# The last 256 tokens of a two-layer trunk: residual by unit-matrix products, output as token rows, and a 7-operation root

## The chip, the cores and the metric

The kernel runs on one core of a Trainium2 chip. A core has a matrix engine (TensorE, PE in the profile; its weight loads are PEld), three elementwise engines (VectorE = DVE, ScalarE = ACT, GpSimd = POOL), and DMA queues, which here are fed by the sync engine (SP) and by POOL. Matrix products are written to banks of PSUM, everything else lies in SBUF on 128 partitions. The metric is the time of one execution in microseconds (us), as the median of several runs.

## The reference

One sequence of 512 tokens with 1024 features passes two layers and a final norm.

```python
for layer in range(2):
    h = rms_norm(x, ln1[layer])
    # layer 0: RWKV-7 time mixing, 12 heads of 64; layer 1: chunk attention, 12 heads
    # both: 4 heads of attention into 256 memory tokens, on rms_norm(mem, mem_norm)
    x = x + concatenate([mix, mo]) @ w_out[layer]
    x = x + conv_glu(rms_norm(x, ln2[layer]), ffn_in[layer], ..., ffn_out[layer])
return rms_norm(x, ln_f)     # x * rsqrt(mean(x * x) + 1e-6) * ln_f
```

`conv_glu` is a gated unit with a three-tap convolution over tokens: (gelu(conv(gate)) * val) @ ffn_out, with 2816 inner features, which are 22 tiles of 128.

## The kernel before

**Layout.** Activations stand with features on partitions: `xT` holds 8 tiles (`KD`) of 128 features x 512 tokens (`S`). A weight is loaded as float32 (`wraw`, two buffers), copied by ACT into a rounded high part `whi` (L170), and DVE (L178) makes the low part `wlo` by subtraction. `dense` then issues three kinds of products into one bank: high x high (L216), high weight x low activation (L217), and, at the end of the bank's series, low weight x high activation (L220).

**Norms.** `acc` collects the squares of the tiles. `norm_steps` multiplies 128-token blocks of it with a matrix of 1/1024 (L270), which puts the mean of each token on a partition, adds 1e-6 (L272), takes the reciprocal root, copies each root along 128 columns (L278), turns the blocks on PE (L283), and copies the result from the bank to `rho` (L284), in which every partition holds the factor of each token. `rsqrt_small` (L237 to L245) starts from an integer estimate and does three Newton rounds of three operations, ten DVE operations in all. `head_rsqrt` does the same for the norms of the heads in layer 0 (sums L906, copy L912, turn L915). The norm of the memory rows (`mrc`, L275) goes through `norm_steps` as well.

**Order.** The work is written as generators, which `weave` interleaves by stated costs; a scheduler with its own model of the engines then fixes the order of the instructions on each engine. Layer 0 runs in stages of 128 mixer features (`prepare`): projections, head norm of the keys, the operands `AR` and `KB` (L991, L995, L999) and 16 pairs of score products from them (L1005). The scores leave over SP by DMA, come back as `Lr`, and after the scan's small products as `Tc` (L1051), which L1144 and L1153 use. The first stage's score products stand next to the keys and values of memory (L884 to L886). The feed-forward parts are held in the order in which they are written.

**The end.** `finish` makes the last feature tile in two halves of 256 tokens. `half(u)` is one series of products into a 128x256 bank. `store(u)` multiplies the bank by `rho` (L1662), adds it to `xT` (L1663), squares on ACT (L1665), scales by `ln_f` on ACT (L1666), adds the squares to `acc` (L1667), runs the norm of these 256 tokens (`norm_rho`), and makes four output tiles of two feature tiles each (L1674), each sent by a DMA on SP (L1676). The store of the first half is woven into the products of the second, and the second store comes after them. The output in memory has partition, feature tile and token as its axes, and the host turns it.

## Time and profile before

| | |
|---|---|
| time, median of 3 runs | 1323.93 us (1323.37 to 1325.35) |
| the profiled execution's own time | 1325.66 us |
| its span | 1323.9 us |
| mean granted TensorE clock | 0.996 |
| PE busy | 1293.9 us, 98% of the span |
| DVE busy | 982.2 us, 74% |
| ACT busy | 787.5 us, 59% |
| POOL busy | 113.4 us, 9% |
| DMA traffic | 170.51 MB, mean 129 GB/s |

The busy time of an engine is the sum of its instructions, and it says nothing of which of them the end waited for. The chain of waits does: it starts at the last instruction and goes back, step by step, to whatever released it. A bracket behind an instruction, as in "[2.16 <-DVE tmp L278]", says that its engine had been idle for 2.16 us and that the copy L278 into a `tmp` tile on VectorE ended the wait. The table by stretches cuts the span into pieces of time and gives each engine's busy time in each of them, with the granted clock as a share of full speed. Groups of instructions give the count, the busy sum and the mean in ns of one.

### The profile page before, as it was taken

The numbers are of one execution on the slowest core, as the hardware profiler recorded it, in microseconds if no ns is written. First come the engines' busy times: TensorE is split into PE (matmuls) and PEld (weight loads), VectorE is DVE, ScalarE is ACT, GpSimd is POOL, SyncE is SP. The second block draws the span as 40 slices with busy tenths as digits, with TensorE's granted clock in tenths as the row PEclk, the third lists the DMA queues.
The fourth block names the chain that finished last, engine by engine and source line by source line (L and its number), as shares of the span: only waits on it lengthen the run. The fifth ranks groups of instructions, "written<-read, shape, count | busy, mean of one in ns | idle before, by whom it ended". The sixth has DMA issues, their size and how long they took to land.

```text
span 1323.9 us, 26431 instructions
## 1 busy us (share of the span) xinstructions
PE 1293.9 (98%) x10558; PEld 1121.0 (85%) x10558; DVE 982.2 (74%) x1947; ACT 787.5 (59%) x1316; POOL 113.4 (9%) x133
## 2 busy tenths in 40 slices
PE   9999999999999999999999999999999999999996
PEld 7787777777789999998888878786899999988886
DVE  7967767765699999998344675757989999995335
ACT  6666665665566666777223566657757667674221
POOL 0000000000001211210000000000012112110000
PEclk9999999999999999999999999999999999999998
DMA  6374434451326887775333432332448878854332
GB/s 199 109 189 98 102 81 110 90 113 57 111 81 160 194 187 178 191 160 143 104 105 102 134 104 72 96 112 72 127 114 193 183 174 201 183 129 128 101 88 78
DMA packets 88683, 170.51 MB, mean 129 GB/s; under 512 B 21232, under 2 KB 31600, under 8 KB 88560
## 3 DMA queue, kind: packets, MB, share of 16 engines
q1 hardware_dynamic: 68320, 124.94, 30.7%
q0 software_dynamic: 20240, 43.88, 19.8%
q8 instruction: 83, 1.36, 0.4%
q14 instruction: 40, 0.33, 0.1%
HBM read 152.57 MB, written 6.29 MB: 120 GB/s over the span
## 4 chain that ended last, share of the span: by engine, by line
PE 80%; DVE 6%; ACT 6%; issue 5%; DMA 3%; SPq 0%; POOL 0%; DVEq 0%; ACTq 0%; POOLq 0%
PE psf L393 19%; PE psd L220 11%; PE psd L216 11%; PE psd L217 11%; PE psf L395 9%; PE pss L1570 1%; DMA wlo<-in_ffn_out_dram 1%; PE pss L906 1%; PE pss L1229 1%; PE pss L1240 1%; PE pss L329 1%; PE pss L1556 1%; PE pss L1379 1%; PE pss L1095 1%; PE pss L319 1%
## 5 line engine op out<-in xcount | busy, mean ns | idle before, releaser
L170 ACT CAST whi<-wraw 128x1024 fp32r<-128x1024 f32 (+1 forms) x116 | 118.0, 1020 | 207.8 <-DMA wraw<-in_ffn_out_dram 130.0
L178 DVE TENSOR_TENSOR wlo<-wraw,whi 128x1024 fp32r<-128x1024 f32 (+1 forms) x93 | 109.6, 1179 | 134.0 <-PE psd L220 70.4
L447 ACT CAST whi<-raw 128x1024 fp32r<-128x1024 f32 (+1 forms) x168 | 153.3, 941 | 68.3 <-PE psf L393 31.9
L393 PE MATMUL psf<-tl,whi 128*128 128x256 f32 x672 | 168.8, 283 | 0.0
L393 PE MATMUL psf<-th,whi 128*128 128x256 f32 x672 | 168.6, 283 | 0.0
L452 DVE TENSOR_TENSOR wlo<-raw,whi 128x1024 fp32r<-128x1024 f32 (+1 forms) x126 | 131.5, 1043 | 14.4 <-ACT whi L447 14.1
L393 PEld LDWEIGHTS psf<-tl,whi 128*128 128x128 f32 x672 | 128.9, 192 | 0.0
L393 PEld LDWEIGHTS psf<-th,whi 128*128 128x128 f32 x672 | 128.7, 192 | 0.0
L216 PE MATMUL psd<-r1h,whi 128*128 128x512 f32 x248 | 101.5, 410 | 0.1
L217 PE MATMUL psd<-r1l,whi 128*128 128x512 f32 x248 | 97.8, 395 | 0.0
L395 PE MATMUL psf<-th,wlo 128*128 128x256 f32 x504 | 81.7, 283 | 0.0
L220 PE MATMUL psd<-r1h,wlo 128*128 128x512 f32 x248 | 72.0, 406 | 0.0
L395 PEld LDWEIGHTS psf<-th,wlo 128*128 128x128 f32 x504 | 69.8, 192 | 0.0
L430 POOL DMA_DIRECT2D wlv<-in_ffn_in_dram x40 | 61.3, 1531 | 58.5 <-DVE tmp L514 57.8
L393 PE MATMUL psf<-r1h,whi 128*128 128x256 f32 x252 | 63.5, 284 | 0.7 <-ACT whi L447 0.7
L393 PE MATMUL psf<-r2h,whi 128*128 128x256 f32 x252 | 63.5, 284 | 0.7 <-ACT whi L447 0.7
L393 PE MATMUL psf<-r1l,whi 128*128 128x256 f32 x252 | 63.2, 283 | 0.0
L393 PE MATMUL psf<-r2l,whi 128*128 128x256 f32 x252 | 63.2, 283 | 0.0
L473 ACT ACTIVATE tmp<-tmp,vec 128x512 f32<-128x512 f32 x44 | 35.9, 817 | 37.9 <-DVE tmp L460 36.6
L216 PEld LDWEIGHTS psd<-r1h,whi 128*128 128x128 f32 x248 | 46.6, 188 | 11.9 <-issue 2.8
L217 PEld LDWEIGHTS psd<-r1l,whi 128*128 128x128 f32 x248 | 46.6, 188 | 8.0 <-issue 0.2
L216 PE MATMUL psd<-th,whi 128*128 128x512 f32 (+1 forms) x136 | 51.0, 379 | 2.3 <-ACT whi L170 2.3
(487 smaller groups left out, 3464.8 us busy)
## 6 DMA issues: line engine op xcount, KB each, us to landing
raw<-in_ffn_in_dram SPq DMA_DIRECT2D x42, 512.0 KB, 3.9
raw<-in_ffn_in_dram SPq DMA_DIRECT2D x84, 256.0 KB, 4.3
wlv<-in_ffn_in_dram POOLq DMA_DIRECT2D x40, 512.0 KB, 8.0
wraw<-in_ffn_out_dram SPq DMA_DIRECT2D x32, 448.0 KB, 3.5
wraw<-in_wA_dram SPq DMA_DIRECT2D x20, 512.0 KB, 4.1
wraw<-in_w_out_dram SPq DMA_DIRECT2D x16, 512.0 KB, 3.9
wraw<-in_ffn_out_dram SPq DMA_DIRECT2D x16, 512.0 KB, 3.5
wlo<-in_wA_dram POOLq DMA_DIRECT2D x15, 512.0 KB, 6.6
```

The costliest lines, as they stand in the source:

```text
L170: high = lambda: pin(SC.copy(hi[:, :n], raw))
L178: pin(V.tensor_tensor(lo[:, :n], raw, hi[:, :n], op=ALU.subtract))
L216: PE.matmul(ps, wh[:, j * P:(j + 1) * P], ah, start=start and n == 0, stop=False)
L217: dense_at[0] = PE.matmul(ps, wh[:, j * P:(j + 1) * P], al, start=False, stop=False)
L220: dense_at[0] = PE.matmul(ps, wl[:, j * P:(j + 1) * P], act(k)[0], start=False, stop=stop and n == len(ks) - 1)
L319: PE.transpose(ps[:, qt * P:(qt + 1) * P], prs[f, hh, qt // 2][:, o:o + P], C("ident"))
L393: PE.matmul(ps, wh[:, o + k * P:o + k * P + P], x[k][n], start=k == n == 0, stop=False)
L395: PE.matmul(ps, wl[:, ol + k * P:ol + k * P + P], x[k][0], start=False, stop=k == 3)
L430: GP.dma_start(self.low[:].rearrange("p (a s) -> p a s", a=2), self.second, accum_op=ALU.add)
L447: keep(SC.copy(hi[:, :n], self.pair(what) if n > S else self.raw[:, what]))
L452: keep(V.tensor_tensor(lo[:, :n], self.pair(what) if n > S else self.raw[:, what], hi[:, :n], op=ALU.subtract))
L473: keep(SC.activation(self.c[:], self.g[:], AF.Identity, scale=Vc(f"cw2_{l}", self.j), bias=Vc(f"cb_{l}", self.j)))
```

## The change

Two things change.

**The root.** `rsqrt_small` keeps the integer estimate and puts one polynomial step in place of the three Newton rounds, so seven DVE operations stand where ten stood. This holds for all norms: the four full ones, the memory's, the two of the halves, and the twelve of the heads.

**The end of the last half.** The residual tile of the second half is divided by `rho` beforehand (L1668, L1669), split in a high and a low part, and added to the bank by two products with a unit matrix (L1676, L1677) at the start of `half(1)`. The bank then holds the new `x` divided by `rho`. The sums over the feature tiles 0 to 6 of these tokens are made within the stream of products (L1702) and kept as `early`, multiplied by the mean that belongs to `rho`, as the squares of the divided bank need it; `na` and `nr` keep the mean and the root of the norm that made `rho`. After the last product ACT squares straight from the bank (L1711), DVE makes `y`, the last output tile without its final factor (L1712), and PE sums the squares (L1722) and turns all eight feature tiles of the two blocks of 128 tokens (L1716), which puts tokens on partitions, into four banks. The final factor is then one number for each partition. ACT scales the first 512 features of a block out of the bank (L1734), DVE the second 512 (L1736), and each piece goes out by its own DMA on SP, in rows of 2 KB. The output is flat: its first half is as before, and its second half has token rows. The store of the first half keeps its operations, but its norm no longer overwrites `rho`.

```diff
+RS_K = 0.7232077432987396
+RS_B, RS_C = -0.653698263378653, 0.8934251408618696
+RS_D, RS_E = -3.069160394934084, 2.756275598910502
...
-    def rsqrt_small(pool, a, n):
-        r = pool.tile([P, 8], F32, name="rsq", tag="rsq")
-        q = pool.tile([P, 8], F32, name="rsq2", tag="rsq2")
-        V.tensor_scalar(r[:, :n].bitcast(I32), a.bitcast(I32), -0.5, 1597463007.0, op0=ALU.mult, op1=ALU.add)
-        for _ in range(3):
-            V.tensor_tensor(q[:, :n], r[:, :n], r[:, :n], op=ALU.mult)
-            V.scalar_tensor_tensor(q[:, :n], q[:, :n], -0.5, a, op0=ALU.mult, op1=ALU.mult)
-            V.scalar_tensor_tensor(r[:, :n], q[:, :n], 1.5, r[:, :n], op0=ALU.add, op1=ALU.mult)
+    def rsqrt_small(pool, a, n, r=None):
+        if r is None:
+            r = pool.tile([P, 8], F32, name="rsq", tag="rsq")
+        y, q, u = (pool.tile([P, 8], F32, name="rsq" + x, tag="rsq" + x) for x in "yqu")
+        y, q, u, r_ = y[:, :n], q[:, :n], u[:, :n], r[:, :n]
+        V.tensor_scalar(y.bitcast(I32), a.bitcast(I32), -0.5, 1597463007.0, op0=ALU.mult, op1=ALU.add)
+        V.tensor_tensor(q, y, y, op=ALU.mult)
+        V.scalar_tensor_tensor(q, q, RS_K, a, op0=ALU.mult, op1=ALU.mult)
+        V.scalar_tensor_tensor(u, q, RS_B, q, op0=ALU.add, op1=ALU.mult)
+        V.scalar_tensor_tensor(q, q, RS_D, q, op0=ALU.add, op1=ALU.mult)
+        V.scalar_tensor_tensor(y, u, RS_C, y, op0=ALU.add, op1=ALU.mult)
+        V.scalar_tensor_tensor(r_, q, RS_E, y, op0=ALU.add, op1=ALU.mult)
         return r
...
+    na, nr = (cp.tile([P, 8], F32, name=n_) for n_ in ("na", "nr"))
+
+    def norm_steps(acc_, rho_, n=4, rc_=None, tied=False, apart=False, into=(None, None)):
...
-        a = cp.tile([P, 8], F32, name="rha", tag="rha")
+        a = into[0] or cp.tile([P, 8], F32, name="rha", tag="rha")
         V.tensor_scalar(a[:, :n], ps[:, 0:2 * n:2], RMS_EPS, None, op0=ALU.add)
-        r = rsqrt_small(cp, a[:, :n], n)
+        r = rsqrt_small(cp, a[:, :n], n, into[1])
...
-        norm = norm_steps(acc, rho[:], apart=True)
+        norm = norm_steps(acc, rho[:], apart=True, into=(na, nr))
...
+    halves = out.rearrange("(h n) -> h n", h=2)
+    outs = (halves[0].rearrange("(p k t) -> p k t", p=P, k=KD), halves[1].rearrange("(t p d) -> t p d", t=2, p=P))
...
+            pss = [None, None]
+            identr = hp.tile([P, P], F32R, name="identr")
+            SC.copy(identr[:], C("ident"))
+            xq = tmp()
+            xh, xl = (tmp(F32R) for _ in range(2))
+            V.reciprocal(xq[:, 256:], rho[:, hts[1]])
+            V.tensor_tensor(xq[:, :256], xT[:, m, hts[1]], xq[:, 256:], op=ALU.mult)
+            split_to(xh[:, :256], xl[:, :256], xq[:, :256])
+            early = cp.tile([P, 4], F32, name="early")
 
             def half(u):
                 ps = pss[u] = ps_d((P, 256))
-                yield from dense(ps[:], us, lambda k: tuple(t[:, hts[u]] for t in hid(k)))
-
-            def store(u):
-                ht = hts[u]
+                if u:
+                    PE.matmul(ps[:], identr[:], xh[:, :256], start=True, stop=False)
+                    PE.matmul(ps[:], identr[:], xl[:, :256], start=False, stop=False)
+                    yield 240
+                yield from dense(ps[:], us, lambda k: tuple(t[:, hts[u]] for t in hid(k)), start=not u)
+
+            def store():
+                ht = hts[0]
                 x_ = xT[:, m, ht]
                 o = tmp()
-                V.tensor_tensor(o[:, :256], pss[u][:], rho[:, ht], op=ALU.mult)
+                V.tensor_tensor(o[:, :256], pss[0][:], rho[:, ht], op=ALU.mult)
                 V.tensor_tensor(x_, x_, o[:, :256], op=ALU.add)
                 sq = tmp()
                 SC.activation(sq[:, :256], x_, AF.Square)
                 SC.activation(x_, x_, AF.Copy, scale=Vc("ln_f", m))
                 V.tensor_tensor(acc[:, ht], acc[:, ht], sq[:, :256], op=ALU.add)
                 yield 2000
-                norm_rho(acc[:, ht], rho[:, ht], 2)
+                norm_rho(acc[:, ht], o[:, 256:], 2)
                 yield 4000
                 for g in range(0, KD, 2):
-                    o = tmp()
-                    ov = o[:].rearrange("p (m t) -> p m t", m=2)
-                    V.tensor_tensor(ov, xT[:, g:g + 2, ht], rho[:, ht].unsqueeze(1).to_broadcast([P, 2, 256]),
+                    w = tmp()
+                    wv = w[:].rearrange("p (m t) -> p m t", m=2)
+                    V.tensor_tensor(wv, xT[:, g:g + 2, ht], o[:, 256:].unsqueeze(1).to_broadcast([P, 2, 256]),
                                     op=ALU.mult)
-                    nc.sync.dma_start(out[:, g:g + 2, ht], ov)
-
-            pss = {}
+                    nc.sync.dma_start(outs[0][:, g:g + 2], wv)
+                ps = ps_s()
+                for t in range(2):
+                    PE.matmul(ps[:, 2 * t:2 * t + 2], acc[:, 256 + t * P:256 + (t + 1) * P], C("ones_d"), start=True, stop=True)
+                V.scalar_tensor_tensor(early[:, 0:2], ps[:, 0:4:2], RMS_EPS, na[:, 2:4], op0=ALU.add, op1=ALU.mult)
+                V.tensor_tensor(early[:, 2:4], na[:, 2:4], nr[:, 2:4], op=ALU.mult)
+                yield 300
+
             run(half(0))
-            weave([(half(1), 22 * 648), (store(0), 12000)])
-            run(store(1))
+            weave([(half(1), 22 * 648), (store(), 12000)])
+            ps, ht = pss[1], hts[1]
+            sq, y = tmp(), tmp()
+            SC.activation(sq[:, :256], ps[:], AF.Square)
+            V.scalar_tensor_tensor(y[:, :256], ps[:], Vc("ln_f", m), rho[:, ht], op0=ALU.mult, op1=ALU.mult)
+            pt = [[ps_f() for _ in range(2)] for _ in range(2)]
+
+            def turn(src, t, k):
+                PE.transpose(pt[t][k // 4][:, k % 4 * P:(k % 4 + 1) * P], src, C("ident"))
+
+            for k in range(4):
+                turn(xT[:, k, 256:256 + P], 0, k)
+            pq = ps_s()
+            for t in range(2):
+                PE.matmul(pq[:, 2 * t:2 * t + 2], sq[:, t * P:(t + 1) * P], C("ones_d"), start=True, stop=True)
+            for t in range(2):
+                for k in range(0 if t else 4, KD - 1):
+                    turn(xT[:, k, 256 + t * P:256 + (t + 1) * P], t, k)
+            for t in range(2):
+                turn(y[:, t * P:(t + 1) * P], t, m)
+            a, f = (cp.tile([P, 8], F32, name=n_) for n_ in ("fa", "ff"))
+            V.tensor_tensor(a[:, :2], pq[:, 0:4:2], early[:, 0:2], op=ALU.add)
+            r_ = rsqrt_small(cp, a[:, :2], 2)
+            V.tensor_tensor(f[:, :2], r_[:, :2], early[:, 2:4], op=ALU.mult)
+            for t in range(2):
+                o = wp.tile([P, 1024], F32, name="wraw", tag="wraw", bufs=2)
+                SC.activation(o[:, :S], pt[t][0][:], AF.Copy, scale=f[:, t:t + 1])
+                nc.sync.dma_start(outs[1][t, :, :S], o[:, :S])
+                V.tensor_scalar(o[:, S:], pt[t][1][:], f[:, t:t + 1], None, op0=ALU.mult)
+                nc.sync.dma_start(outs[1][t, :, S:], o[:, S:])
```

The shorter root changes the order on the engines in layer 0. In the first stage (25 to 66 us of the profile before), VectorE's rows up to the operand `KB` of the first score products read, before and after (`rsq_523` and `rsq_524` are the root of the keys' head norm, `rsq_540` that of the memory norm, `wlo_650`, `wlo_692`, `wlo_649` low parts of weights):

```order
L244 SCALAR_TENSOR_TENSOR rsq_540<-rsq2_541,rsq_540 128x2
L912 COPY tmp_559<-rsq_523 128x512
L242 TENSOR_TENSOR rsq2_541<-rsq_540 128x2
L243 SCALAR_TENSOR_TENSOR rsq2_541<-rsq2_541,rha_538 128x2
L244 SCALAR_TENSOR_TENSOR rsq_540<-rsq2_541,rsq_540 128x2
L275 COPY mrc_139<-rsq_540 128x2
L990 TENSOR_TENSOR kn_327<-kn_327,pss_561 128x512
L178 TENSOR_TENSOR wlo_692<-wraw_689,whi_691 128x1024
L991 TENSOR_TENSOR AR_325<-kn_327,E_91 128x8x64
L993 SCALAR_TENSOR_TENSOR tmp_568<-a_320,kn_327 128x512
L278 COPY tmp_575<-rsq_540 128x256
L995 SCALAR_TENSOR_TENSOR KB_324<-tmp_568,Ei_323 128x8x64
```
```order
L249 SCALAR_TENSOR_TENSOR rsqq_542<-rsqq_542 128x2
L250 SCALAR_TENSOR_TENSOR rsqy_541<-rsqu_543,rsqy_541 128x2
L920 COPY tmp_558<-rsq_524 128x512
L251 SCALAR_TENSOR_TENSOR rsq_540<-rsqq_542,rsqy_541 128x2
L181 TENSOR_TENSOR wlo_649<-wraw_646,whi_648 128x1024
L283 COPY mrc_141<-rsq_540 128x2
L998 TENSOR_TENSOR kn_328<-kn_328,pss_560 128x512
L999 TENSOR_TENSOR AR_326<-kn_328,E_93 128x8x64
L1001 SCALAR_TENSOR_TENSOR tmp_567<-a_321,kn_328 128x512
L286 COPY tmp_574<-rsq_540 128x256
L1003 SCALAR_TENSOR_TENSOR KB_325<-tmp_567,Ei_324 128x8x64
```

Between the copies L912 and L920 and `KB`, three root operations and the subtraction of L178 on `wlo_692` stood before; now one root operation and a subtraction of an earlier weight (`wlo_649`, which stood two rows ahead of the first fence) stand there, and the subtraction of `wlo_692`'s counterpart, `wlo_691`, comes six rows after L1003. On PE the sixteen pairs of L1005, which stood together, become thirteen and, after 36 memory products, three.

In the later stages of layer 0 the head norm stands on VectorE like this, before and after (`rsq_2035` and `rsq_2032` are its root, `bon` the bonus term):

```order
L243 SCALAR_TENSOR_TENSOR rsq2_2036<-rsq2_2036,hra_2033 128x8
L244 SCALAR_TENSOR_TENSOR rsq_2035<-rsq2_2036,rsq_2035 128x8
L961 SCALAR_TENSOR_TENSOR v_2049<-tmp_2047,vec_67,v_2049 128x511
L242 TENSOR_TENSOR rsq2_2036<-rsq_2035 128x8
L1080 TENSOR_TENSOR bon_1480<-pss_2052,v_2049 128x512
L243 SCALAR_TENSOR_TENSOR rsq2_2036<-rsq2_2036,hra_2033 128x8
L244 SCALAR_TENSOR_TENSOR rsq_2035<-rsq2_2036,rsq_2035 128x8
L912 COPY tmp_2056<-rsq_2035 128x512
L1028 TENSOR_TENSOR Xu_1847<-Lr_1842,cst_66 128x120
```
```order
L248 SCALAR_TENSOR_TENSOR rsqu_2035<-rsqq_2034 128x8
L249 SCALAR_TENSOR_TENSOR rsqq_2034<-rsqq_2034 128x8
L250 SCALAR_TENSOR_TENSOR rsqy_2033<-rsqu_2035,rsqy_2033 128x8
L251 SCALAR_TENSOR_TENSOR rsq_2032<-rsqq_2034,rsqy_2033 128x8
L969 SCALAR_TENSOR_TENSOR v_2045<-tmp_2043,vec_67,v_2045 128x511
L920 COPY tmp_2052<-rsq_2032 128x512
L1088 TENSOR_TENSOR bon_1478<-pss_2048,v_2045 128x512
L1293 TENSOR_TENSOR tmp_1999<-tmp_1999,pss_2054 128x512
L1036 TENSOR_TENSOR Xu_1844<-Lr_1839,cst_66 128x120
```

The copy for the turn stood behind `bon`, and now stands ahead of it. On PE the turn itself (L915, now L923) stands five products nearer to the sums of its norm.

The end of TensorE's program, before and after (`hl`, `th`, `r2l` and `sl` are parts of the inner activations, `psd`, `psf` and `pss` banks):

```order
L216 MATMUL psd<-r2l,whi 128x256
L217 MATMUL psd<-sl,whi 128x256
L220 MATMUL psd<-hl,wlo 128x256 x7
L220 MATMUL psd<-th,wlo 128x256 x8
L220 MATMUL psd<-r2l,wlo 128x256 x7
L270 MATMUL pss<-cst,acc 128x2 x2
L283 MATMUL pss<-cst,tmp 128x128 x2
```
```order
L219 MATMUL psd<-r2l,whi 128x256
L220 MATMUL psd<-sl,whi 128x256
L223 MATMUL psd<-hl,wlo 128x256 x7
L223 MATMUL psd<-th,wlo 128x256 x8
L223 MATMUL psd<-r2l,wlo 128x256 x7
L1716 MATMUL psf<-cst,xT 128x128 x4
L1722 MATMUL pss<-cst,tmp 128x2 x2
L1716 MATMUL psf<-cst,xT 128x128 x10
L1716 MATMUL psf<-cst,tmp 128x128 x2
```

Behind the last low products stood two sums and two turns of the root; now four turns of output tiles, two sums, ten more turns and the two of `y` stand there. The early sums (L1702) stand among the products, five pairs of L219 and L220 ahead of the first row of the second piece.

More of the change, by code (lines that the diff above doesn't have):

```diff
@@ L262, in trunk_kernel @@
     norm_at = [None]
-    def norm_steps(acc_, rho_, n=4, rc_=None, tied=False, apart=False):
+    na, nr = (cp.tile([P, 8], F32, name=n_) for n_ in ("na", "nr"))
+    def norm_steps(acc_, rho_, n=4, rc_=None, tied=False, apart=False, into=(None, None)):
         if tied:
@@ L1763 @@
         aps[name] = nc.dram_tensor(f"in_{name}_dram", a.shape, _mybir.dt.from_np(a.dtype), kind="ExternalInput").ap()
-    out = nc.dram_tensor("out_0_dram", (P, KD, S), F32, kind="ExternalOutput").ap()
+    out = nc.dram_tensor("out_0_dram", (S * KD * P,), F32, kind="ExternalOutput").ap()
     with _tile.TileContext(nc) as tc:
@@ L1768 @@
     got = r.results[0]["out_0_dram"]
-    return np.ascontiguousarray(got.transpose(2, 1, 0).reshape(1, S, KD * P))
+    first, second = got.reshape(2, -1)
+    first = first.reshape(P, KD, S // 2).transpose(2, 1, 0).reshape(S // 2, KD * P)
+    return np.concatenate([first, second.reshape(S // 2, KD * P)])[None]
```

## The prediction

> **What bounds the kernel now.** I read the page first, then the time table by stretches, then the chain of waits, then single instructions at the two places where the chain leaves TensorE.
>
> ```profile
> span 1323.9 us, 26431 instructions
> PE 1293.9 (98%) x10558; PEld 1121.0 (85%) x10558; DVE 982.2 (74%) x1947; ACT 787.5 (59%) x1316; POOL 113.4 (9%) x133
> PE 80%; DVE 6%; ACT 6%; issue 5%; DMA 3%; SPq 0%; POOL 0%; DVEq 0%; ACTq 0%; POOLq 0%
> ```
>
> TensorE is busy for 98% of the span and carries 80% of the chain. A change that adds or removes VectorE work therefore counts only where TensorE stands still, so I ask in which stretches it does (columns: stretch, length, busy PE, PEld, DVE, ACT, POOL, granted clock, DMA share, GB/s):
>
> ```profile
> 30.00:60.00 30.00, 27.70 (x150) 22.74 (x150) 28.20 (x65) 17.33 (x29) 0.31 (x1) 1.00 0.36 104
> 60.00:100.00 40.00, 39.38 (x357) 34.62 (x356) 27.50 (x71) 24.59 (x40) 1.86 (x2) 0.96 0.64 170
> 400.00:700.00 300.00, 297.53 (x2108) 280.25 (x2107) 245.96 (x360) 181.50 (x240) 43.97 (x42) 1.00 0.67 160
> 1312.00:1324.00 12.00, 1.17 (x6) 0.75 (x6) 5.41 (x18) 1.29 (x3) 0.00 (x0) 0.70 0.34 115
> ```
>
> The feed-forward stretch (400 to 700) has 297.5 of 300 us of PE: the 7-operation root buys nothing there. From 30 to 60 DVE is the full engine (28.2 of 30) and PE has 2.3 us idle; at the end PE works 1.17 of 12 us. The change can pay in these two places.
>
> **The end of the last half: 2.4 us gained.** The first two rows are of the chain (start, length, what), the others single instructions (in brackets: idle before, and who ended it).
>
> ```profile
> 1308.86 2.65 PE psd L220 x22
> 1317.71 0.69 DVE tmp L1674
> ```
> ```profile
> 1311.53 0.42 DVE L1662 TENSOR_TENSOR tmp<-psd,rho 128x256 f32<-128x256 f32 x1 [0.81 <-PE psd L220]
> 1312.45 0.42 ACT L1665 ACTIVATE tmp<-xT 128x256 f32<-128x256 f32 x1 [4.26 <-DVE xT L1663]
> 1312.90 0.43 DVE L1667 TENSOR_TENSOR acc<-acc,tmp 128x256 f32<-128x256 f32 x1 [0.48 <-ACT tmp L1665]
> 1313.47 0.58 PE L270 MATMUL pss<-cst,acc 128*128 128x2 f32 x4 [1.97 <-DVE acc L1667]
> 1314.08 0.16 DVE L272 TENSOR_SCALAR rha<-pss 128x2 f32<-128x2 f32 x1 [0.76 <-PE pss L270]
> 1314.28 0.17 DVE L240 TENSOR_SCALAR rsq<-rha 128x2 int32<-128x2 int32 x1
> 1316.24 0.29 DVE L278 COPY tmp<-rsq 128x256 f32<-128x256 f32 x1
> 1316.68 0.59 PE L283 MATMUL pss<-cst,tmp 128*128 128x128 f32 x2 [2.64 <-DVE tmp L278]
> 1317.31 0.37 ACT L284 COPY rho<-pss 128x256 f32<-128x256 f32 x1 [3.91 <-PE pss L283]
> ```
>
> From the release of the last products (1311.53) to the first stored tile (1317.71 + 0.69 = 1318.40) pass 6.87 us, all of them one after the other. The change takes out the multiply and the add of the residual, the add to `acc`, the copy, the turn and the copy out of the bank, and three root operations. What stays or comes:
>
> - In the PE stream, ahead of the last product: two identity products at 2.65 / 22 = 0.12 each, and the early sums, 0.58 as the L270 row. Together 0.82, all of it on the path, since PE has no gap there.
> - Behind the last product: Square 0.42, hand-over 0.14 (1312.90 + 0.43 to 1313.47), sums 0.58, hand-over 0.03, nine small DVE operations (add, seven of the root, multiply), hand-over 0.04 (1316.68 + 0.59 to 1317.31), and the scaled 128x512 read of the bank on ACT. The ten root operations took 1316.24 - 1314.28 = 1.96, so 0.196 each and 1.76 for nine. The nearest row for the scaled read (L945):
>
> ```profile
> L945 ACT ACTIVATE tmp<-pss,aw0h 128x512 f32<-128x512 f32 x6 | 4.1, 684 | 0.5 <-PE pss L940 0.4
> ```
>
> 0.42 + 0.14 + 0.58 + 0.03 + 1.76 + 0.04 + 0.68 = 3.65. The gain is 6.87 - 0.82 - 3.65 = 2.40; if the early sums cost no more than their two issue slots of 0.12 it is 2.74.
>
> The sixteen turns of blocks must fit beside this. Four lie ahead of the sums, so they run during Square. By the row of L915 below (0.60 for four, 0.15 each) the other twelve take 1.80, from 1.14 (end of the sums) to 2.94 after the last product; the scale factors are there at 2.97. They fit, with nothing to spare for the second bank: if a turn cost the 0.295 of L283's row, the second bank would be 1.7 late, the first not, and the second transfer would start about 1.0 later than the first one ends. That bounds the gain from below at 1.4.
>
> Then the stores. Four transfers carry 1.05 MB before and after:
>
> ```profile
> 11.00:12.00 1.00, 1.00 (x4) 0.60 (x4) 0.74 (x2) 1.00 (x3) 0.00 (x0) 1.00 1.10 438
> 1320.00:1321.00 1.00, 0.00 (x0) 0.00 (x0) 0.21 (x1) 0.00 (x0) 0.00 (x0) 0.50 1.03 339
> ```
>
> At the end they flow at 339 GB/s, 3.09 us, 0.77 a transfer; tiles come every 0.6 to 0.7 us, so the flow, not the engines, sets the pace in both kernels. The rows get longer (2 KB instead of 1 KB), which no row here prices for stores: between nothing and the 438 GB/s of loads at the start (2.39 us, a further 0.70). I take nothing, because the nearer row is the store's own. [...]
>
> The reciprocal, residual split and `y` cost nothing: DVE idles 3.92 us just before it may start on the first half, as row L1662 of that half shows; without that cover three operations at its 0.43 would add about 1.3.
>
> ```profile
> 1302.34 0.43 DVE L1662 TENSOR_TENSOR tmp<-psd,rho 128x256 f32<-128x256 f32 x1 [3.92 <-PE psd L220]
> ```
>
> **The first stage, 55 to 66 us: 2.9 us gained.** Here the shorter root re-sorts VectorE's rows.
>
> ```profile
> 57.15 1.22 DVE L178 TENSOR_TENSOR wlo<-wraw,whi 128x1024 fp32r<-128x1024 f32 x1
> 58.29 0.69 DVE L991 TENSOR_TENSOR AR<-kn,E 128x512 f32<-128x512 f32 x1
> 59.69 0.69 DVE L995 SCALAR_TENSOR_TENSOR KB<-tmp,Ei 128x512 f32<-128x512 f32 x1
> ```
> ```profile
> 55.91 0.60 PE L915 MATMUL pss<-cst,tmp 128*128 128x128 f32 x4
> 56.26 1.41 PE L220 MATMUL psd<-r1h,wlo 128*128 128x512 f32 x5
> 59.83 0.44 PE L283 MATMUL pss<-cst,tmp 128*128 128x128 f32 x2 [2.16 <-DVE tmp L278]
> 60.52 1.88 PE L1005 MATMUL pss<-KB,AR 64*64 64x64 f32 x32 [0.25 <-DVE KB L995]
> 62.71 0.41 PE L885 MATMUL psl<-whi,ML 128*128 128x256 f32 x1
> 64.28 0.28 PE L884 MATMUL psl<-whi,ML 128*128 128x256 f32 x1
> 64.39 0.28 PE L885 MATMUL psl<-whi,ML 128*128 128x256 f32 x1
> 104.55 1.15 PE L1005 MATMUL pss<-KB,AR 64*64 64x64 f32 x32
> ```
>
> PE runs out of products at 57.67 (56.26 + 1.41), waits 2.16 for the copy L278, then 0.25 for `KB`, which DVE finishes at 60.38. Ahead of `KB` DVE loses three operations of the first norm's root (0.59 at 0.196), six of the head and memory norms (0.9, at the 0.16 that L272's row takes, less a little overlap; bounds 0.6 and 1.2), and one lo-part subtraction, which moves behind `KB` (58.29 - 57.15 = 1.14). `KB` is ready 2.63 earlier, at 57.75. On PE one lo product and three of the sixteen score pairs move behind this point (0.23 and 0.20 which must be done later), so of the 2.63 remain 2.2.
>
> The wait also lowers the clock (windows):
>
> ```profile
> 62.00:64.00 2.00, 2.00 (x16) 1.88 (x14) 2.00 (x4) 1.46 (x5) 0.00 (x0) 0.50 0.04 4
> 64.00:66.00 2.00, 2.00 (x19) 2.00 (x19) 1.90 (x3) 0.61 (x1) 0.00 (x0) 0.98 0.17 17
> ```
>
> At 0.50 the score products took 1.88 against 1.15 later (0.73), and the eight products from 62.71 to 64.28 took 1.57 against 8 x 0.11 (0.69): 1.42 for the clock. I count half of it, 0.7: the moved subtraction holds its weight buffer, so the next memory weights are loaded and cast later, and part of the earlier start will be waited for there. 2.2 + 0.7 = 2.9, between 2.2 and 3.6. [...]
>
> What is late next: the three score pairs now stand behind 36 memory products (36 x 0.11 = 4.0 us), and through them the scan's transfers on SP and their result `Tc`.
>
> ```profile
> 94.23 1.76 SPq L1051 DMA_DIRECT2D Tc<-d2a  x4
> 106.19 0.44 DVE L1144 STREAM_TRANSPOSE Tn<-Tc 128x256 f32<-128x256 f32 x1
> ```
>
> `Tc` is issued by 95.99 and first used at 106.19: about 8 us of cover, 4 after the change. Then nothing waits; without cover the cost would be the 4.0.
>
> **The later head norms: 0.** In three further stages the turn of the norm (L915) moves five products (5 x 0.23 = 1.15) up in PE's order, while its copy is earlier by three root operations and by `bon`, which now comes behind it:
>
> ```profile
> 155.10 0.69 DVE L1080 TENSOR_TENSOR bon<-pss,v 128x512 f32<-128x512 f32 x1
> 156.10 0.43 DVE L912 COPY tmp<-rsq 128x512 f32<-128x512 f32 x1
> 156.58 0.65 PE L915 MATMUL pss<-cst,tmp 128*128 128x128 f32 x4
> ```
>
> 3 x 0.2 + 0.61 (the step from L1080 to the next row) = 1.2, so the two cancel; bounds: 0.4 gained in all, or 3 x 1.15 = 3.45 lost if the copy does not come earlier.
>
> **Sum.** 2.4 + 2.9 = 5.3 us. The profiled execution took 1325.66, 1.73 above the median of 1323.93; its next would be 1320.4, and the median 1318.6.
>
> **The rivals.**
>
> - *More than that.* Stores at the loads' rate (0.70) and the whole clock term (0.72): 6.7, so 1317.2. For it: 438 GB/s exists in this trace. Against: no store here has reached it.
> - *Only the end gains.* The memory weights arrive too late and PE waits in the first stage as before, a little further on: 2.4, so 1321.5, give or take 1. For it: from 60 to 100 PE has only 0.62 idle, each engine is near its limit, and a weight cast stands behind the moved subtraction.
> - *Nothing gained in all*, because sums, turns and the second bank delay the end and the front gives its gain back: 1323.9.
> - *Slower.* The turned norm waits. In the three later stages PE reaches L915's place 1.15 early, and if the scheduler's subtraction of 1.14 sits ahead of the copy as well, PE stands 2.3 us, about what lowered the clock at 59.83. Each stage then costs 2.3 + 1.42 (the clock) = 3.7, three 11.2; less 5.3 leaves 5.9 lost: 1329.8. It decides once the wait at L915's successor passes some 2.1 us in these stages. Against it: the copy should come 1.2 earlier.
>
> **How the numbers follow.** Forecast 0.51 (own range 1317.4 to 1319.8); more 0.12; only the end 0.22; nothing 0.06; slower 0.09. A measurement of this kernel can tell about 0.2%, 2.65 us, from no change: faster means below 1321.28, slower above 1326.58. The first two cases and four tenths of the third are faster: 0.51 + 0.12 + 0.09 = 0.72; the rest of the third and the fourth are the same: 0.13 + 0.06 = 0.19; slower 0.09. The range runs from 1316.4 (more, with the 0.34 of cheaper early sums and 0.4 of the head norms on top) to 1322.6 (upper end of the third case); outside lie the last two cases and a little below, 0.18.
>
> **What would show it.** Right: between the last lo product and the first ACT scale some 2.9 to 3.1 us, no PE wait over 0.5 near 58 us and a clock near 1.00 from 60 to 66, the same PE time from 400 to 1290. Wrong: a PE wait of over 1 us between 60 and 100 on a weight cast, on `Tc` or on the three late score pairs; idle time over 0.5 at the turned head norms near 150, 195 and 240 us; output transfers that start more than 4 us after the last product, or wait for the second bank.

## The result, and the profile after

The changed kernel takes 1330.76 us (median of 22 runs, 1322.52 to 1335.46); the kernel before, on the same chips, 1324.84 (22 runs, 1322.94 to 1328.49). The ratio over all executions is 1.0033, with a 95% interval from 1.0018 to 1.0049 (that of the two medians is 1.0045): slightly slower, where 5.3 us less was forecast. The median hides two groups: 7 executions lie between 1322.5 and 1325.0, 15 between 1330.3 and 1335.5, and nothing between them. The mean granted clock is 0.998 to 0.999 in the shorter ones and 0.990 to 0.993 in the longer ones. The profile is of a shorter one (1323.34, span 1321.6).

The page of the changed kernel and its table by stretches, to be held against those of before (stretch, length, busy PE, PEld, DVE, ACT, POOL, clock, DMA share, GB/s):

```profile
span 1321.6 us, 26416 instructions
PE 1298.2 (98%) x10578; PEld 1120.4 (85%) x10578; DVE 973.5 (74%) x1891; ACT 788.7 (60%) x1318; POOL 112.6 (9%) x133
```
```profile
30.00:60.00 30.00, 29.17 (x179) 24.09 (x179) 28.03 (x61) 18.05 (x31) 0.31 (x1) 1.00 0.35 101
60.00:100.00 40.00, 39.05 (x337) 33.81 (x337) 27.28 (x67) 23.98 (x38) 1.86 (x2) 1.00 0.63 170
62.00:64.00 2.00, 2.00 (x19) 1.92 (x17) 1.80 (x3) 0.00 (x0) 0.00 (x0) 1.00 0.39 100
```

From 30 to 60 us TensorE has 0.83 us idle, where it had 2.30, and the clock from 62 to 64 is 1.00, where it was 0.50. VectorE's and TensorE's timelines in the first stage:

```profile
57.32 0.68 DVE L1003 SCALAR_TENSOR_TENSOR KB<-tmp,Ei 128x512 f32<-128x512 f32 x1
```
```profile
58.80 1.02 PE L1013 MATMUL pss<-KB,AR 64*64 64x64 f32 x26
64.04 0.44 PE L1013 MATMUL pss<-KB,AR 64*64 64x64 f32 x6
67.25 0.38 PE L219 MATMUL psl<-ML,whi 128*128 128x256 f32 x1 [0.95 <-ACT vm L897]
```

`KB` is there at 58.00 (forecast 57.75) and the score products start at 58.80 instead of 60.52. At 66 us TensorE leads the kernel before by 3.4 us; the three late pairs and a wait of 0.95 for ScalarE bring that down to 1.8 at 69, and at 120 it leads by 2.0.

The end of the changed kernel: two rows of its chain of waits (start, length, what), the timelines of ScalarE, TensorE and VectorE, and a stretch of the stores:

```profile
1308.45 0.34 PE pss L1702 x4
1310.33 2.64 PE psd L223 x22
```
```profile
1313.01 0.38 ACT L1711 ACTIVATE tmp<-psd 128x256 f32<-128x256 f32 x1 [4.63 <-PE psd L223]
1313.44 0.61 PE L1722 MATMUL pss<-cst,tmp 128*128 128x2 f32 x4
1313.91 1.29 PE L1716 MATMUL psf<-cst,xT 128*128 128x128 f32 x10
1314.09 0.16 DVE L1729 TENSOR_TENSOR fa<-pss,early 128x2 f32<-128x2 f32 x1 [0.18 <-PE pss L1722]
1315.04 0.38 PE L1716 MATMUL psf<-cst,tmp 128*128 128x128 f32 x2
1315.78 1.27 ACT L1734 ACTIVATE wraw<-psf,ff 128x512 f32<-128x512 f32 x2 [2.39 <-DVE ff L1731]
```
```profile
1319.00:1320.00 1.00, 0.00 (x0) 0.00 (x0) 0.00 (x0) 0.00 (x0) 0.00 (x0) 0.94 1.03 389
```

The last products are done at 1312.97 and the first scaled piece at about 1316.42 (half of 1.27 after 1315.78): 3.45 us, forecast 3.65. The turns are ready at 1315.42, before the factors. The early sums cost 0.34 instead of 0.58, and the stores flow at 389 GB/s instead of 339. From the last product to the end of the span pass 8.63 us, before 12.37, which is 3.74 less; the early sums (0.34) and the two identity products (0.12 each) take 0.58 of that back in the stream, and the end gains 3.2, forecast 2.4.

So both places gain. The loss lies where nothing was looked for. Up to 308 us the changed kernel leads by 1.5; from 312 on it is 0.5 behind, so it has lost 2.0:

```profile
308.09 0.56 PE L1265 MATMUL psl<-ML,VT 128*64 128x64 f32 x11
310.39 0.98 PE L1265 MATMUL psl<-ML,VT 128*64 128x64 f32 x21 [1.74 <-issue]
```

These rows are of the profile of a longer execution (below); the shorter one has the same wait at the same product. 32 products on operands that are all there stop after the eleventh, and the profile names no semaphore ("issue"). In the kernel before the same 32 are one block:

```profile
309.86 1.15 PE L1257 MATMUL psl<-ML,VT 128*64 128x64 f32 x32
```

From 345 to 392 us and from 640 to 745 the changed kernel then falls back a further 1.1 and 1.5 us, at a steady 1 to 3%, with no wait in the trace. From 900 to 1290 it regains 2.1, and at 1290 it is 0.9 behind; with the 3.2 of the end this gives the 2.3 us by which its span is the shorter one.

### The profile page after: what moved, and what is told of

It is laid out like the page before. It is cut to its first block, busy times and chain, and to the rows that moved or that the text cites. A ratio compares the mean times of both kernels' runs of the same rounds, so it can differ in the third digit from the quotient of the medians.

```text
span 1321.6 us, 26416 instructions
## 1 busy us (share of the span) xinstructions
PE 1298.2 (98%) x10578; PEld 1120.4 (85%) x10578; DVE 973.5 (74%) x1891; ACT 788.7 (60%) x1318; POOL 112.6 (9%) x133
## 3 DMA queue, kind: packets, MB, share of 16 engines
q8 instruction: 83, 1.36, 0.4%
## 4 chain that ended last, share of the span: by engine, by line
PE 78%; ACT 8%; DVE 7%; issue 4%; DMA 3%; SPq 0%; DVEq 0%; ACTq 0%; POOL 0%; POOLq 0%
PE psf L401 16%; PE psd L219 12%; PE psd L220 11%; PE psd L223 11%; PE psf L403 8%; PE pss L1578 1%; ACT whi L173 1%; PE pss L914 1%; DMA wraw<-in_ffn_in_dram 1%; PE pss L1237 1%; ACT whi L455 1%; PE pss L1248 1%; DMA wlv<-in_ffn_in_dram 1%; DVE raw L442 1%; PE pss L1103 1%
## 5 line engine op out<-in xcount | busy, mean ns | idle before, releaser
L219 PE MATMUL psd<-r1h,whi 128*128 128x512 f32 x248 | 102.8, 415 | 0.0
L220 PE MATMUL psd<-r1l,whi 128*128 128x512 f32 x248 | 98.8, 398 | 0.0
L219 PEld LDWEIGHTS psd<-r1h,whi 128*128 128x128 f32 x248 | 46.5, 188 | 12.7 <-issue 2.7
L220 PEld LDWEIGHTS psd<-r1l,whi 128*128 128x128 f32 x248 | 46.6, 188 | 9.1 <-issue 0.8
L219 PE MATMUL psd<-th,whi 128*128 128x512 f32 (+1 forms) x136 | 51.1, 380 | 2.3 <-ACT whi L173 2.3
```

Of the source, the lines that this page charges most:

```text
L219: PE.matmul(ps, wh[:, j * P:(j + 1) * P], ah, start=start and n == 0, stop=False)
L220: dense_at[0] = PE.matmul(ps, wh[:, j * P:(j + 1) * P], al, start=False, stop=False)
```

## The experiments

All edits are to the changed kernel unless a kernel is named. The kernel before ran beside each (medians 1324.84 to 1325.10).

**The parts apart.** First the changed kernel unaltered (e1), then each of its two parts: e2 is the kernel before with the `rsqrt_small` of the changed kernel, e3 the changed kernel with the `rsqrt_small` of the kernel before.

> The changed kernel once more, unaltered, for a profile of one of its longer executions and for the granted clock of every execution. Theory C (the clock): its executions fall in two groups, near 1323 us at a mean clock of 0.999 and near 1331 us at 0.991; in a long one the profile shows some 20 us at half clock in one place, about 310 us, where the first profile has a TensorE wait of 1.74 us and a 3.4 us window with 49% of TensorE busy. Rival E (the end): the long executions lose their 8 us after 1290 us, in the new products, turns or stores. Rival F (feed-forward): they lose it evenly at full clock, 0.8% everywhere.

> Only the 7-operation root, with the old end. VectorE's and TensorE's order up to the last feature tile is that of the changed kernel. Theory C: two groups again, near 1326.5 (1323.3 and the 3.2 us that the new end took less in the profile) and near 1334.5, about two thirds in the longer one. Rival E: one group, near 1326. The forecast on record would have it 2.9 us under before, at about 1321.9.

> Only the new end, with the old 10-operation root; the order up to the last feature tile is that of the kernel before. Theory C: one group, no execution at a clock under 0.995, and a gain of 3.2 us less three root operations at 0.2, so 2.6 us: about 1322.2 against 1324.8. Rival E: two groups, the longer one near 1331.

Measured: e1 1327.98 (12 runs; six from 1321.8 to 1325.1, six from 1330.9 to 1333.7), ratio 1.0016 (0.9995 to 1.0037). e2 1333.68 (6 runs: one at 1325.0, five from 1333.1 to 1336.4), ratio 1.0058 (1.0035 to 1.0081). e3 1324.93 (11 runs, one group, clock 0.996 to 0.999), ratio 1.0004 (0.9995 to 1.0012). The two groups belong to the root. The new end is innocent of them, but the 2.6 us did not show either. The profile of e1 is of a longer execution; its table around the wait, and the same stretches in the shorter profile:

```profile
307.50:311.00 3.50, 1.76 (x34) 1.22 (x33) 2.77 (x5) 2.94 (x8) 0.00 (x0) 1.00 0.35 136
311.00:314.40 3.40, 3.40 (x16) 2.26 (x11) 1.29 (x2) 0.00 (x0) 0.00 (x0) 0.50 0.02 5
314.40:317.80 3.40, 3.40 (x15) 2.26 (x14) 1.57 (x3) 1.15 (x5) 0.00 (x0) 0.50 0.00 0
324.60:328.00 3.40, 3.40 (x24) 2.65 (x24) 1.38 (x4) 1.36 (x6) 0.00 (x0) 0.50 0.11 45
```
```profile
307.50:311.00 3.50, 1.76 (x27) 1.19 (x28) 2.71 (x5) 3.18 (x9) 0.00 (x0) 1.00 0.39 149
311.00:314.40 3.40, 3.40 (x36) 2.40 (x31) 1.96 (x5) 0.29 (x1) 0.00 (x0) 1.00 0.02 5
314.40:317.80 3.40, 3.40 (x87) 2.79 (x86) 2.84 (x9) 2.75 (x11) 0.00 (x0) 1.00 0.01 2
```

Both executions wait alike, and TensorE is busy for 1.76 of 3.5 us. Behind the wait the clock falls to 0.50 in the one and not in the other: from 310.97 to 328.03, 17.07 us, in which e1 does half the work; the two spans differ by 7.7 us. (e2's profile has the same, for 20.48 us.) That the granted clock makes the groups is shown; why a given execution falls into one is not.

e3 shows the same uncertainty at the place where the kernel before has its half clock. It has the old order there and the same waits of 2.16 and 0.25, but its clock stays at 1.00, and the 32 score products that took 1.88 take 1.15 (TensorE's timeline and a stretch, both of e3):

```profile
59.74 0.44 PE L288 MATMUL pss<-cst,tmp 128*128 128x128 f32 x2 [2.16 <-DVE tmp L283]
60.43 1.15 PE L1010 MATMUL pss<-KB,AR 64*64 64x64 f32 x32 [0.25 <-DVE KB L1000]
```
```profile
60.00:62.00 2.00, 1.45 (x35) 1.17 (x34) 2.00 (x5) 1.76 (x4) 0.00 (x0) 1.00 0.50 201
```

So here too the clock fell behind a wait (2.16 us) in the one profile and stayed at 1.00 behind the same wait in the other.

**The wait: instruction fetch.** The trace also has the packets by which instructions are fetched: on the page's list of queues, 83 packets and 1.36 MB on one queue, so 16 KB each.

```profile
q8 instruction: 83, 1.36, 0.4%
```

TensorE's 21,290 instructions in the trace (21,156 weight loads and products, the rest waits on semaphores and the like) make some 256 for each packet. Counted through the trace, the wait begins behind number 7873 in all nine profiles with the shorter root whose program is not shifted, and the packet that is due near number 7611 comes late (in the changed kernel the one before it starts at number 7355, at 294.81 us). What the queues carried meanwhile stands in SP's timeline, first of before, then of the changed kernel, and in the table by stretches, in the same order:

```profile
289.32 0.33 SPq L189 DMA_DIRECT2D wraw<-in_w_out_dram  x1
```
```profile
302.77 0.50 SPq L192 DMA_DIRECT2D wraw<-in_w_out_dram  x1
```
```profile
306.00:308.00 2.00, 2.00 (x82) 1.57 (x78) 1.04 (x2) 0.67 (x3) 0.00 (x0) 1.00 0.04 8
```
```profile
306.00:308.00 2.00, 2.00 (x70) 1.45 (x70) 0.06 (x1) 1.98 (x5) 0.00 (x0) 1.00 1.08 413
```

The re-sorting put one 512 KB weight load behind the scan's transfers on SP. From 306 to 308 the DMA engines moved 8 GB/s before and 413 after, and the packet of instructions, due at 304.96, starts at 308.12, near the end of these transfers. Two edits test this: to move the program against the fetches, and to move the load.

```diff
-    for _ in range(6):
+    for _ in range(2):
         PE.matmul(idle[:, 0:256], zeros[:, 0:P], zeros[:, 0:256], start=True, stop=True)
+    for _ in range(36):
+        PE.matmul(idle[:, 0:32], zeros[:, 0:P], zeros[:, 0:32], start=True, stop=True)
```

> The changed kernel; the only edit is in TensorE's idle loop before the first weights arrive: four of its six products of 256 columns become 36 of 32 columns. The loop takes about as long, but every later TensorE instruction moves 128 places (64 weight loads and 64 products) further on in the program. Theory F (instruction fetch): the 16 KB fetch that was due at TensorE's instruction 7611 (305.0 us) waited behind data transfers until 308.0, and TensorE ran dry 256 instructions on, inside L1265. Shifted, the fetch is due at about 301.5 us, ahead of these transfers: the 1.7 us wait inside L1265 goes, no half clock of 17 us follows, all executions fall in one group, about 1323.3 - 1.7 = 1321.6 us. Rival S (a semaphore or a bank): the wait stays inside L1265 between the same products, with two groups of times as before.

```diff
-    def raw_w(src, n=1024):
+    def raw_w(src, n=1024, gate=None):
         raw = wp.tile([P, 1024], F32, name="wraw", tag="wraw", bufs=2)
+        if gate is not None:
+            V.tensor_copy(raw[:, 0:1], gate)
         nc.sync.dma_start(raw[:, :n], src)
...
-                w = load_w(A["w_out"][l, m])
+                gate = act(3)[0][:, 0:1] if (l, m) == (0, 3) else None
+                w = load_w(A["w_out"][l, m], gate=gate)
```

> The changed kernel with its TensorE program unmoved; one weight load (the fourth tile of the first output projection, 512 KB) gets one more condition, a copy of one column into its buffer by VectorE, so that it no longer starts at 302.8 us but after 313. Theory F: the transfers of 302 to 308 us end about 2 us sooner, the fetch due at 305.0 is served in time, the wait inside L1265 falls from 1.74 to under 0.5 us, one group of times near 1321.6 us, unless the later load is waited for in the projection (then up to 3 us more, as a wait on its cast near 360 us). Rival S: wait and groups stay.

Measured: e4 1339.06 (4 runs), ratio 1.0112 (1.0098 to 1.0127). The loop was mis-sized: 72 passes took 15.41 us, and everything comes some 12 us later. The wait inside the 32 products is gone, as theory F had it, and TensorE gains 2.0 us there on the changed kernel; but other series of tiny products now break off elsewhere, at 119.7, 204 and 247 us. Behind the first of them the clock is at 0.50 from 122.1 to 125.5 (TensorE's timeline in e4):

```profile
121.02 0.23 PE L1180 MATMUL pss<-Y,Tn 16*16 16x16 f32 x7 [1.11 <-issue]
...
324.13 1.15 PE L1267 MATMUL psl<-ML,VT 128*64 128x64 f32 x32
```

All three stops lie a whole multiple of 256 instructions ahead of number 7873. The wait goes with the place of the instructions in the program, not with the operands: rival S is out. As a time e4 says nothing, since its loop is 12 us too long.

e5 1322.01 (11 runs, 1320.5 to 1325.5), ratio 0.9984 (0.9974 to 0.9994). The group above 1330 is gone; the clock is 0.997 and above. One group it is not: six executions at a clock of 0.999 or more lie between 1320.5 and 1322.0, five at 0.997 to 0.998 between 1323.7 and 1325.5. The load goes out at 319.41, and the wait falls from 1.74 to 0.90, where under 0.5 was expected (TensorE's timeline in e5):

```profile
311.51 0.85 PE L1268 MATMUL psl<-ML,VT 128*64 128x64 f32 x21 [0.90 <-issue]
```

What is left of the wait stands behind the 1 MB that `flush_mix` reads back from 301.67 on; that this causes the rest was not tried. In the five profiles with the later load (e5, e8, e10, e11, e12) the wait is still 0.82 to 1.43 us and the packet 2.5 to 3.1 us behind number 7611, against 3.1 to 3.3 with the load in its way, so the load is the smaller part of the delay. The times of the fetch in five of the profiles, in us:

```
kernel                 no. 7611 runs   packet starts   no. 7874 runs   behind the packet
before                     306.46          307.0         (no wait)
changed, longer (e1)       304.71          308.0          310.39            2.4
later load (e5)            306.66          309.2          311.51            2.3
both remedies (e8)         307.70          310.6          312.89            2.3
root, later load (e10)     303.81          306.3          308.61            2.3
```

TensorE goes on 2.3 to 2.4 us after the late packet has started in these four, 2.25 to 2.5 in all nine, and stops some 256 instructions behind the place where it was due. In the kernel before that would be 309.3, before number 7874 runs at 310.15: no wait there.

The kernel before has such a stop too, in another place: behind number 7361, which is 512 ahead of 7873, at 296.5 us, and it goes on 2.4 us after a packet that started at 295.32. Its profile puts this wait down to a copy on ScalarE, but in the changed kernel the same products start ahead of that copy's end. The three other profiles with the old root (e3, e6, e9) stop there as well.

```profile
295.90 0.83 PE L1109 MATMUL pss<-cst,KB 64*128 64x64 f32 x16
297.71 1.53 PE L1229 MATMUL pss<-VT,Tt 64*64 64x128 f32 x24 [0.98 <-ACT ML L1112]
```

**The steady loss: addresses.** The new small tiles lie ahead of the weight buffers in SBUF, and nearly everything above them moves up: by 224 bytes per partition in the changed kernel, 64 with the root alone, 160 with the end alone. An unused tile gives the kernel before such a shift (e6, 160 bytes, shown here), or rounds that of the changed kernel up (e7, the same lines with `[P, 8]`, 32 bytes).

```diff
     norm_at = [None]
+    cp_pad = cp.tile([P, 40], F32, name="pad")
+    GP.memset(cp_pad[:, 0:1], 0.0)
```

> The kernel before with one unused tile of 160 bytes per partition ahead of the weight buffers, so that everything above it in SBUF lies 160 bytes higher, as in the kernel with only the new end. Theory A (addresses): the products on the low part r1l take 233 instead of 227 ns, from 350 to 395 and from 640 to 745 us, and those on hl 231; the time rises by about 1.5 us to 1326.4. Rival N: no effect, 1324.9; the slower products of the changed kernels then have another cause.

> The changed kernel with one unused tile of 32 bytes per partition, which makes its shift of the SBUF addresses against the kernel before 256 instead of 224 bytes. Theory A with a period of 256 bytes or less: the products on r1l and hl are back at 227 ns and the shorter group falls by about 1.5 us, to 1321.8. Theory A with a longer period, or rival N: they stay at 231 to 234 ns, 1323.3. In all cases two groups, since TensorE's program and the loads are unmoved.

Measured: e6 1328.23 (5 runs), ratio 1.0031 (1.0019 to 1.0043): 3.2 us more, with not an instruction of the computation changed or moved. In its profile, which is of the longest execution, 2.6 us are lost from 345 us on, where the slower products stand, and 2.0 before that, most of it ahead of 100 us, for which no cause was found. e7 1327.14 (12 runs), ratio 1.0013 (0.9997 to 1.0028): three from 1320.7 to 1321.0, nine from 1326.3 to 1331.2, so both groups lie 2.5 to 3 us under those of the changed kernel. The groups by shape from 655 to 735 us, in order: before, e6, changed, e7 (busy, then mean ns of one):

```profile
L216 PE MATMUL psd<-r1l,whi 128*128 128x512 f32 x42 | 16.3, 389 | 0.0
L220 PE MATMUL psd<-hl,wlo 128*128 128x512 f32 x42 | 10.5, 389 | 0.0
```
```profile
L216 PE MATMUL psd<-r1l,whi 128*128 128x512 f32 x38 | 15.0, 396 | 0.0
L220 PE MATMUL psd<-hl,wlo 128*128 128x512 f32 x35 | 8.9, 394 | 0.0
```
```profile
L219 PE MATMUL psd<-r1l,whi 128*128 128x512 f32 x42 | 16.7, 397 | 0.0
L223 PE MATMUL psd<-hl,wlo 128*128 128x512 f32 x35 | 8.9, 394 | 0.0
```
```profile
L219 PE MATMUL psd<-r1l,whi 128*128 128x512 f32 x42 | 16.4, 389 | 0.0
L223 PE MATMUL psd<-hl,wlo 128*128 128x512 f32 x42 | 10.5, 389 | 0.0
```

389 ns at shifts of 0 and 256 bytes, 394 to 397 at 160 and 224. In the spacing of successive products that is 227 against 231 to 234 ns. Products of `whi` with `th` and `tl`, which were shifted by as much, stay at 227. As built, `r1h` and `r1l` lie below the new tiles and keep their addresses in all these kernels; their products slow down when the weights' buffers move, so it is not the streamed operand's own address that does it. Products on `hl`, which moved with the weights, are slower too, by 2 to 5 ns, so the distance between weight and operand alone does not settle it. That the addresses do it is shown; by what is not.

**Both remedies, and the parts at equal addresses.** e8 is the changed kernel with e5's later load and e7's 32 bytes; e9 the end alone (e3) with 96 bytes; e10 the root alone (e2) with the later load and 192 bytes. All three then lie 256 bytes up. e11 and e12 are e8 and e10 once more.

> The changed kernel with both remedies: the later weight load and the 32 bytes that make the shift of the addresses 256. If the two costs are independent, the median is that of the later load alone, 1322.0, less the 2.5 us by which the 32 bytes lowered the shorter group (1323.3 to 1320.8): 1319.5, one group, products on r1l at 227 ns. That is 5.4 us under before, the 5.3 of the forecast. If they are not independent: 1322.

> Only the new end, old root, with 96 unused bytes per partition, so that the addresses lie 256 instead of 160 bytes above those of the kernel before. Theory A: with the products back at 227 ns the gain of the end shows: with three root operations more than the changed kernel 2.4 - 0.6 = 1.8 by the forecast, 2.6 by the profile of the unpadded kernel, so 1322.3 to 1323.1 against 1324.9. Rival N: 1324.9, as unpadded.

> Only the 7-operation root, old end, with the later weight load and 192 unused bytes (again 256 in all): what the re-sorted order is worth by itself. By the forecast 2.9 plus three operations at the old end 0.6, so 1321.4; by the first profile of the changed kernel, where TensorE led by 3.4 us at 66 us, by 1.8 at 69 and by 2.0 at 120, 2.0 plus 0.6: 1322.3. If the order is worth nothing: 1324.3.

> The changed kernel with the later load and the 32 bytes once more, for more executions: its first series missed the sum of the two parts by some 2 us (2.8 for the end and 3.9 for the root would give 1318.4), and its profile shows the clock at 0.50 from 48.9 to 55.7 us. If that half clock strikes in some executions only, the times spread again from 1318.5 (mean clock 0.998 or more) to 1323.5 (0.996), median about 1320.5. If the first series was an accident, 1318.4.

> The root alone with the later load and the 192 bytes once more; the program of the first 300 us is the one of the kernel beside it. If the half clock near 49 us belongs to that order, some executions here have it too and lie 2 to 3 us above the others (1321 to 1324); the first six did not show it. If they again don't, 1321.2, and the cause is not the order alone.

| | runs | median, us | ratio to before | interval |
|---|---|---|---|---|
| e8, both remedies | 6 | 1320.55 | 0.9966 | 0.9953 to 0.9980 |
| e11, the same | 5 | 1319.83 | 0.9958 | 0.9945 to 0.9972 |
| e9, end alone, 256 bytes | 11 | 1322.30 | 0.9978 | 0.9969 to 0.9987 |
| e10, root alone, later load, 256 bytes | 6 | 1321.18 | 0.9970 | 0.9959 to 0.9981 |
| e12, the same | 10 | 1321.83 | 0.9979 | 0.9970 to 0.9988 |

The end is worth 2.8 us (1325.10 to 1322.30, with three root operations more than the changed kernel), the root 3.9 and 3.1 in its two series. Both together give 4.6 and 5.1, so e8 and e11 beat both kernels on record, but by some 1.5 less than the sum. Most of what is missing goes with the clock. Four executions of e8 and e11 have a mean clock of 0.999 or more, and they take 1318.5 to 1319.8 us, near the 1318.4 to 1319.2 that the sum of the parts would give; the other seven take 1319.6 to 1323.5. Both profiles are of the others and have the clock at half near 49 us, behind a stretch (44.3 to 47.7) in which TensorE is busy for 2.7 and 2.6 of 3.4 us, before 3.26. The rows are of e8 and e10:

```profile
48.90:55.70 6.80, 6.80 (x33) 6.80 (x33) 5.73 (x23) 2.19 (x3) 0.00 (x0) 0.50 0.55 160
```
```profile
48.90:55.70 6.80, 6.80 (x51) 6.37 (x50) 6.32 (x24) 3.90 (x5) 0.00 (x0) 1.00 0.52 173
```

The profiles of e5 and e7 have the half clock there too, for 3.41 us. e10 and e12 have the same order there and the same sparse stretch, without the half clock in either profile, and so have both profiles of the changed kernel; so the order alone does not decide it, and what does stays open. Nor does the length of a wait: with 1.45 us near 310 us in its profile e7 has nine long executions of twelve, and with 1.43 near 308 e12 has none above 1325.1.

## Why the prediction was wrong, point by point

- **The end** (2.4): right in mechanism. Profiled 3.2, and 2.8 by e9. The mis-sized terms: the early sums were put at the 0.58 of a waiting row and took 0.34 in the stream; the way to the first scaled piece took 0.2 less; the stores were put at no gain and flow at 389 GB/s instead of 339, 0.4 for the 1.05 MB.
- **The first stage** (2.9): right in mechanism; 2.0 profiled at 120 us. `KB` was 0.25 later than forecast, and the lead of 3.4 at 66 us shrank by 1.6 at the late pairs and at a wait for ScalarE. The half clock near 61 us is absent, but the row did not show that the wait makes it: e3 has the same wait and a full clock.
- **The later head norms** (0): held; the lead goes from 2.0 us at 120 to 1.5 at 300, and the wait for the turned norm's copy is 0.4 us in all.
- **The step that failed** is "what is late next". It followed the moved instructions on VectorE and TensorE and one chain on SP (`Tc`), but not the order of the weight loads on SP up to the end of layer 0, where one load moved behind fourteen transfers, nor the packets of TensorE's own instructions, of which one, due at 304.96, started at 308.12, with such transfers at 413 GB/s from 306 to 308. It put this at nothing without a reason. The rival "slower" had the right pair, a wait and a half clock behind it, in the wrong place with the wrong cause of the wait: not a turned norm on TensorE, but a late packet of TensorE's own code. One wait cost 2.0 directly (1.74 of it idle) and, in two thirds of the executions, some 8 us more by the clock (medians of the groups 1331.6 and 1323.5), where the prediction had put 1.4 on a lowered clock.
- **The second step that failed** is "the same PE time from 400 to 1290": instructions that neither change nor move were taken to cost what they cost. At the addresses of the changed kernel they took about 2.5 us more (e7), from 345 us on. With both remedies the kernel runs at 1319.8 to 1320.6, inside the range on record (1316.4 to 1322.6), though a part of the wait remains.
- **The sums.** They come out, but for the two bounds, which are each 0.1 wider than their terms give (1316.5 and 1322.5).
- **The clock.** In all profiles with a lowered clock inside the program it lasts 3.41 us or a whole multiple (6.83, 17.07, 20.48). In e1 it fell behind a stretch with TensorE busy for half of it (1.76 of 3.50 us), and stayed down for 17.07 us although TensorE was busy for all of each 3.40 us; in the shorter profile it did not fall behind the same 1.76 of 3.50, and in e3 it did not fall behind a stretch with TensorE busy for 1.00 of 3.41 us. So the idle time ahead of a place does not tell, in these profiles, whether the clock falls there.

## What to carry to other kernels

A change that re-sorts a schedule is to be followed through every queue, the weight loads on SP among them, and not only where its gain lies; a TensorE wait that ends with "issue" in the middle of independent products is a reason to hold the instruction queue's packets against the data transfers. Before two versions are compared, their large buffers are brought to the same addresses, or here 256 bytes apart, the one shift at which no cost was seen: 160 bytes alone cost 3.2 us. Where executions fall in two groups, the granted clock of each tells more than their median.

## What the runs showed of the hardware that was not expected

- TensorE's instructions come in packets of 16 KB, some 256 instructions each, 83 of them (1.36 MB) on a queue of their own in the list of DMA queues. In the changed kernel one that was due at 304.96 us started at 308.12, with 413 GB/s of data from 306 to 308, and TensorE stopped some 256 instructions behind the place where it was due. In the nine profiles with this stop TensorE goes on 2.25 to 2.5 us after the packet has started; the fourteen profiles have sixteen such stops of 0.8 to 2.0 us, all a whole multiple of 256 instructions apart. They stand in series of tiny products, where 256 instructions ran in about 3.6 us (304.71 to 308.3 in e1), against some 18 us in the feed-forward part (4215 in the 300 us from 400 to 700).
- Behind one wait of 1.74 us, in a stretch with TensorE half busy (1.76 of 3.50 us), the granted clock was 0.50 for 17.07 us in one execution (e1; 20.48 in e2's profile) and 1.00 in another of the same program. Behind the 2.16 us of the kernel before it was 0.50 for 3.41 us, and behind the same wait in e3 it stayed at 1.00.
- Unchanged products took another time when SBUF buffers lay elsewhere: those of `r1l` with `whi` and of `hl` with `wlo` 389 ns at shifts of 0 and 256 bytes, 394 to 397 at 160 and 224; those of `th` with `whi` stayed at 389.
